# Half-size loads of the second half's token sums, and the final norm's weights in one VectorE operation, in a hybrid decoder layer

## The chip, the cores and the metric

The kernel runs on one core of a Trainium2 chip. The metric is the device time of one execution in microseconds (us). TensorE is called PE below, VectorE DVE (in the code `V`), ScalarE ACT (`A`), GpSimd POOL (`G`), and SyncE SP; SP issues nearly all DMA transfers. Each engine works through its own instructions in order, and semaphores tie the engines to each other.

## The reference

One decoder layer over 2048 tokens of 1024 features, all in float32. Its first part (a projection, gated linear attention on one group of heads, dilated sliding-window attention on the other, an output projection, residual) gives `h`. The change touches only what follows:

```python
nm = rmsnorm(h, mlp_norm_g[l])
a = jnp.square(jax.nn.relu(jnp.einsum('bsd,df->bsf', nm, w_ff1[l])))   # 1024 -> 4096
h = h + jnp.einsum('bsf,fd->bsd', a, w_ff2[l])                         # 4096 -> 1024
return rmsnorm(h, final_norm_g)       # x * rsqrt(mean(x^2) + 1e-6) * g
```

## The kernel before, in words

**Arithmetic.** Every float32 operand of a large matrix product is split in a high and a low part: `split` (L485 to L487) has ACT copy it to the high part (L486) and DVE subtract that from the original to get the low part (L487). `mm3` (L141 to L144) then adds three matmuls, high·high (L142), low·high (L143) and high·low (L144), each 128x128 by 128x512. The products are block products of Strassen's kind: sums and differences of blocks are formed first, so that a 2x2 block product takes seven multiplications in place of eight.

**MLP1** (L1280 to L1394). The 2048 tokens are worked in two halves. For each half there are 16 groups of 256 hidden features, and in each group seven products in the `order` 1, 2, 6, 5, 7, 3, 4; these 224 are the list `jobs1`. `prep1` forms and splits the weights of a job (tiles `w1raw`, `w1comb`), two jobs ahead. The other operand is one of seven token-sum blocks per half, which stay in SBUF as high and low tiles `hb` (`TF[j]`, each 128x2048) for all 16 groups of the half. A product is added up in a PSUM bank; `ps_a`, `ps_c`, `ps_d` and `ps_o` are the names of eight banks used in turn. When it is done, ACT copies the bank to SBUF (L1371, L1385) or DVE adds it to another (L1373, L1377, L1381), and ACT applies ReLU and square (L1362, L1363, L1386). `some_sums` adds the results for MLP2 on DVE (L1335) and SP stores these sums (L1337, L1368).

**The switch between the halves.** The `hb` tiles hold the seven blocks of one half only. Those of the second half were computed earlier and wait in DRAM (`hTD[1]`). During the last group of the first half (jobs from `first` = 7·15 = 105 on) block after block has been used for the last time, and its tiles are filled again: `reload` (L1246 to L1261) loads a whole block of 128x2048 (1 MB) into one of two `rb` buffers, and the generator that it returns splits the block in two halves of 1024 columns, each by `split`. `parts_at` says after which job each of the 14 half splits stands in the program. The loads of the first two blocks are issued at job `first` − 2, that of block n + 2 when both halves of block n have been split and so its buffer is free.

**MLP2** (L1432 to L1639). 26 products (`PRODUCTS`) of four steps each. Per step, `prep_a` loads and splits activation sums (`ra`, then `ca`; with a negative sign by L1458 and L1459), `prep_b` splits weight sums (`bs`, then `cb`), and `update_b` (L1490 to L1499) adds a freshly loaded weight block (`rb`) to `bs`, mostly on POOL (L1499). L1487 and L1497 load weights, L1446 activations. PE needs the split `ca` and `cb` of a step before its matmuls. `taken` (L1547 to L1561) adds a finished PSUM bank to the output tiles `sum` on DVE (L1556).

**The final norm** (`output`, L1510 to L1523) is called when an output row block of 128 tokens is complete, once for each of 16 row blocks, in four sets of four. A row block is two tiles of 128x512, `C[0]` and `C[1]`. ACT squares both with a running sum (L1515), POOL multiplies `C[0]` with the weights `g` (L1517), ACT makes the row factor `r` (L175, L176, L1518), DVE multiplies `C[1]` with `r` and `g` in one operation (L1520), ACT scales `C[0]` with `r` (L1521), and both tiles are stored (L1522, L1523). `last` is true for the last row block alone.

**Order of the work.** The program is written as above, and a scheduler of the tile framework puts each engine's instructions in their final order before the kernel runs. So an instruction added in one place can change the order of others on its engine; a wait follows from what an instruction reads and writes.

Of the kernel before, what the change touches and what calls it, by code (L numbers as in the profile page):

```python
# [13 lines left out]
AF = mybir.ActivationFunctionType  # L14
OP = mybir.AluOpType
# [101 lines left out]
def emit(tc, a, stop=99):  # L117
    nc = tc.nc
    V, A, G, T, SP = nc.vector, nc.scalar, nc.gpsimd, nc.tensor, nc.sync
# [6 lines left out]
    def ps(tag):  # L126
        return psum.tile([128, 512], F32, name="ps_" + tag, tag=tag, bufs=BANKS[tag])

    def slot(name, dt=F32, n=SLOT):

        return up.tile([128, SLOT], dt, name=name, tag="u", bufs=25)[:, :n]
# [34 lines left out]
    def stat(n=1):  # L166
        if stat_at[0] + n > 48:
            stat_at[0] = 0
        s = stats[:, stat_at[0]:stat_at[0] + n]
        stat_at[0] += n  # L170
        return s

    def rstd_of(ssq, width, n=1, bias=eps):
        r = stat(n)
        A.activation(r, ssq, AF.Ln, bias=bias, scale=1.0 / width)  # L175
        A.activation(r, r, AF.Exp, scale=-0.5)  # L176
        return r
# [46 lines left out]
    hTD = dram.tile([2, 7, 128, 4, 512], F32, name="hTD")  # L224
# [15 lines left out]
    CX, c11, c12, c21, c22, last = [t[:, GP * q:GP * q + GP] for t in acc for q in range(2)]  # L240
# [11 lines left out]
    order = (1, 2, 5, 6, 3, 4, 7)  # L252
# [4 lines left out]
    TF = {j: [slot(f"tb{j}", FR) for _ in range(2 if j < 7 else 1)] for j in order}  # L257
# [227 lines left out]
    def split(hi, lo, src):  # L485
        A.activation(hi, src, AF.Copy)  # L486
        V.tensor_tensor(lo, src, hi.bitcast(F32), op=OP.subtract)  # L487
# [109 lines left out]
    def reload(n):  # L597

        j, cs = order[n // 2], slice(1024 * (n % 2), 1024 * (n % 2) + 1024)
        t = (xp, bp)[n // 2 % 2][:, cs]  # L600
        SP.dma_start(t, nTD[j - 1].rearrange("p c s -> p (c s)")[:, cs])

        def rest():
            hi, lo = [v[:, cs] for v in TF[j]]
            tc.keep_in_program_order(A.activation(hi, t, AF.Copy))
            V.tensor_tensor(lo, t, hi.bitcast(F32), op=OP.subtract)
            if n + 4 < 14:
                back.append(reload(n + 4))

        return rest  # L610
# [121 lines left out]
    for at in range(7, len(jobs)):  # L732
        g = jobs[at][0]
# [419 lines left out]
    for pr in range(4):  # L1153
# [3 lines left out]
        for hh, br in seq:  # L1157
# [3 lines left out]
            first = len(units)  # L1161
# [62 lines left out]
    rb, TF, TB = [slot("rb")], {}, {}  # L1224
# [53 lines left out]
    order = (1, 2, 6, 5, 7, 3, 4)  # L1278
# [10 lines left out]
    def prep1(at):  # L1289

        if at >= len(jobs1):
            return
        g, j = jobs1[at]
        if not combs1:
            combs1.extend(view(c[:, 1024 * q:], (2, 4, 128)) for c in [slot("w1comb", FR) for _ in range(2)]
                          for q in range(2))
        r = raw1[g % 2]
        (a11, a12), (a21, a22) = [[r[:, 4 * k:4 * k + 4, n * 128:n * 128 + 128] for k in range(2)] for n in range(2)]
        c = combs1[at % 4]
        split(c[:, 0], c[:, 1], {1: a11, 2: a12, 6: a11, 5: a21, 7: a11, 3: a12, 4: a22}[j])  # L1300
        if j == 1:
            V.tensor_tensor(a21, a21, a22, op=OP.add)
            V.tensor_tensor(a11, a21, a11, op=OP.subtract)
        if j == 2:
            V.tensor_tensor(a12, a12, a11, op=OP.subtract)
        if j == 6:
            V.tensor_tensor(a11, a22, a11, op=OP.subtract)
        if j == 4:
            load_w1(g + 2)
# [80 lines left out]
    def some_sums(n=3):  # L1390

        for _ in range(n):
            while sums1 and next(sums1[0], 0) == 0:
                sums1.pop(0)  # L1394
# [5 lines left out]
    for at, t in enumerate(tiles):  # L1400
# [8 lines left out]
        p = [ps("a"), ps("a")]  # L1409
        parts_ = 2 if at < 2 else 1  # L1410
        for q in range(parts_):
            for n in range(2):
                cs = slice(n * 512, n * 512 + 512)
# [20 lines left out]
    raw_a, comb_a, raw_b, comb_b, state, fin = [], [], [], [], [], {}  # L1434
# [5 lines left out]
    def load_a(n):  # L1440

        if n < 2 * NPH:
            p, k = divmod(n, 2)
            if len(raw_a) < 2:
                raw_a.append(view(slot("ra"), (4, 512)))
            SP.dma_start(raw_a[n % 2], actD[AT[p], :, 4 * k:4 * k + 4].rearrange("p q h s -> p q (h s)"))  # L1446

    def prep_a(n):

        if n >= LAST:  # L1450
            return
        if len(comb_a) < 3:
            comb_a.append(view(slot("ca", FR), (2, 2, 512)))
        c, r = comb_a[n % 3], raw_a[n // 2 % 2][:, n % 2 * 2:n % 2 * 2 + 2]
        if PRODUCTS[n // 4][0] > 0:
            split(c[:, 0], c[:, 1], r)
        else:
            A.activation(c[:, 0], r, AF.Copy, scale=-1.0)  # L1458
            V.scalar_tensor_tensor(c[:, 1], r, -1.0, c[:, 0].bitcast(F32), op0=OP.mult, op1=OP.subtract)  # L1459
        if n % 2:  # L1460
            load_a(n // 2 + 2)
# [14 lines left out]
    def fetch_b(n):  # L1476

        if n >= LAST:
            return
        if not raw_b:  # L1480
            raw_b.extend(view(v[:, 1024 * e:], (2, 512)) for v in [slot("rb2") for _ in range(2)] for e in range(2))
        fetched[n] = []
        for op, k, m in PRODUCTS[n // 4][2]:
            if op != "=":
                v = raw_b[turns[0] % 4]
                turns[0] += 1
                SP.dma_start(v, w2_part(n, k, m))  # L1487
                fetched[n].append((op, v))

    def update_b(n, engines=(G, V)):  # L1490

        if n >= LAST:
            return
        v = state_of(n)
        for op, k, m in PRODUCTS[n // 4][2]:
            if op == "=":
                SP.dma_start(v, w2_part(n, k, m))  # L1497
        for e, (op, r) in enumerate(fetched.pop(n)):
            engines[e].tensor_tensor(v, v, r, op=OP.add if op == "+" else OP.subtract)  # L1499

    def prep_b(n):

        if n >= LAST:
            return
        if len(comb_b) < 3:
            comb_b.append(view(slot("cb", FR), (2, 2, 512)))
        v = comb_b[n % 3]
        split(v[:, 0], v[:, 1], state_of(n))

    def output(C, row, i, last=False):  # L1510

        scr = fin["scr"][:, 512 * (i % 2):512 * (i % 2) + 512]
        ss, part = stat(2), stat()
        for n in range(2):
            A.activation(scr, C[n], AF.Square, accum_out=ss[:, n:n + 1])  # L1515
            if n == 0:
                G.tensor_tensor(C[0], C[0], fin["g"][:, :512], op=OP.mult)  # L1517
                A.activation(part, ss[:, 0:1], AF.Copy, bias=EPS, scale=1.0 / D)  # L1518
        r = rstd_of(ss[:, 1:2], D, bias=part)
        V.scalar_tensor_tensor(C[1], C[1], r, fin["g"][:, 512:], op0=OP.mult, op1=OP.mult)  # L1520
        A.activation(C[0], C[0], AF.Copy, scale=r)  # L1521
        SP.dma_start(out2[row:row + 128, 512:], C[1])  # L1522
        (A if last else SP).dma_start(out2[row:row + 128, :512], C[0])  # L1523

# [58 lines left out]

    first, parts_at = 7 * (NP - 1), {}
    for n in range(14):
        parts_at.setdefault(first + 1 + n * 4 // 5, []).append(n // 2)
    halves, begun = {}, set()
    for at in range(7, len(jobs1)):
        if at == first - 2:
            halves.update({n: reload(order[n], 1) for n in range(2)})  # L1590
        prep1(at + 2)
        some_sums()
        product1(at)
        for n in parts_at.get(at, ()):
            next(halves[n])
            if n in begun and n + 2 < 7:
                halves[n + 2] = reload(order[n + 2], 1)
            begun.add(n)
        n = at + 6 - len(jobs1)
        if n == 0:  # L1600
            load_a(0)
        if 0 <= n < 4:
            fetch_b(n)
            update_b(n, (V, V))
        if n == 3:
            load_a(1)
        if n in (3, 5):
            prep_b(n // 2 - 1)
            prep_a(n // 2 - 1)
            fetch_b(n // 2 + 3)  # L1610
# [4 lines left out]
    for ph, (_, chained, _, _) in enumerate(PRODUCTS):  # L1615
# [3 lines left out]
        for k in range(4):  # L1619
            n = 4 * ph + k  # L1620
# [53 lines left out]
def build(nc, inputs, stop=99):  # L1674
    arrays, aps = {}, {}
    for name in _INS:
        arrays[name] = np.ascontiguousarray(inputs[name])
    arrays.update(_constants())
    for name, v in arrays.items():
        aps[name] = nc.dram_tensor(name, v.shape, mybir.dt.from_np(v.dtype), kind="ExternalInput").ap()  # L1680
    aps["out"] = nc.dram_tensor("out", (1, S, D), F32, kind="ExternalOutput").ap()
    with tile.TileContext(nc, schedule_with_timeline_sim=True) as tc:
        emit(tc, aps, stop)
    return arrays
# [10 lines left out]
```

## Time and profile before

| what | value |
|---|---|
| median of 3 runs | 2280.32 us (2277.76 to 2281.45) |
| the profiled execution | 2283.21 us |
| its span, first to last instruction | 2281.4 us |
| mean granted PE clock | 0.994 of full speed |
| DVE busy | 1630.4 us (71% of the span) |
| ACT busy | 1230.4 us (54%) |
| POOL busy | 544.3 us (24%) |
| L486, ACT, `hb` from `rb`, 14 splits | 1052 ns each (median) |
| L487, DVE, `hb` from `rb`, 14 splits | 1223 ns each (median) |
| L1521, ACT, 16 scalings | 711 ns each (median) |

A row of a timeline has the start in us, the duration in us, the engine, the line of the kernel, the operation, output and inputs, shapes and the count; a row with a count above 1 stands for neighbours taken together. In square brackets stands how long the engine was idle just before, and what ended it. Busy shares are averages over stages that have different limits, so what counts for the change are the rows at the places that it touches.

### The profile page before, as it was taken

The numbers are of one execution on the slowest core, as the hardware profiler recorded it, in microseconds if no ns is written. First come the engines' busy times: TensorE is split into PE (matmuls) and PEld (weight loads), VectorE is DVE, ScalarE is ACT, GpSimd is POOL, SyncE is SP. The second block draws the span as 40 slices with busy tenths as digits, with TensorE's granted clock in tenths as the row PEclk, the third lists the DMA queues.
The fourth block names the chain that finished last, engine by engine and source line by source line (L and its number), as shares of the span: only waits on it lengthen the run. The fifth ranks groups of instructions, "written<-read, shape, count | busy, mean of one in ns | idle before, by whom it ended". The sixth has DMA issues, their size and how long they took to land.

```text
span 2281.4 us, 35136 instructions
## 1 busy us (share of the span) xinstructions
PE 2249.2 (99%) x12508; PEld 1945.9 (85%) x12508; DVE 1630.4 (71%) x3065; ACT 1230.4 (54%) x2436; POOL 544.3 (24%) x482
## 2 busy tenths in 40 slices
PE   9999999999999999999999999999999999999998
PEld 8978998899999998888888887888888878888876
DVE  8788878766667676446777778777777577576778
ACT  6665436426877874234555556555555433333446
POOL 1210002024385672000000000000007562032465
PEclk9999999999999999999999999999999999999999
DMA  5458754776768864678544456555479988676775
GB/s 201 134 182 245 252 155 136 223 234 221 223 196 255 262 207 139 221 232 273 185 138 153 137 161 202 163 165 163 128 266 285 311 279 277 214 254 227 261 255 175
DMA packets 359920, 478.59 MB, mean 210 GB/s; under 512 B 19333, under 2 KB 268694, under 8 KB 347712
## 3 DMA queue, kind: packets, MB, share of 16 engines
q1 hardware_dynamic: 355246, 467.69, 63.6%
q0 software_dynamic: 4352, 8.39, 2.0%
q8 instruction: 98, 1.61, 0.3%
q14 instruction: 78, 0.64, 0.1%
q10 hardware_dynamic: 146, 0.27, 0.0%
HBM read 326.54 MB, written 154.44 MB: 211 GB/s over the span
## 4 chain that ended last, share of the span: by engine, by line
PE 84%; DMA 5%; POOL 3%; DVE 3%; issue 3%; ACT 2%; SPq 0%; POOLq 0%; ACTq 0%; DVEq 0%
PE ps_a L143 9%; PE ps_a L142 9%; PE ps_a L144 9%; PE ps_c L143 7%; PE ps_c L142 7%; PE ps_c L144 7%; PE ps_a L893 4%; PE ps_o L142 3%; PE ps_o L144 3%; PE ps_o L143 3%; PE ps_d L143 3%; PE ps_d L142 3%; PE ps_d L144 3%; PE ps_d L874 3%; PE ps_c L852 2%
## 5 line engine op out<-in xcount | busy, mean ns | idle before, releaser
L1499 POOL TENSOR_TENSOR bs<-bs,rb 128x1024 f32<-128x1024 f32 x72 | 217.7, 3031 | 1072.3 <-DMA actD<-ring 836.9
L486 ACT ACTIVATE cb<-bs 128x1024 fp32r<-128x1024 f32 x104 | 110.2, 1060 | 272.7 <-issue 116.2
L487 DVE TENSOR_TENSOR cb<-bs,cb 128x1024 fp32r<-128x1024 f32 x104 | 165.2, 1589 | 124.4 <-ACT cb L486 123.7
L487 DVE TENSOR_TENSOR w1comb<-w1raw,w1comb 128x512 fp32r<-128x512 f32 x224 | 153.8, 689 | 96.4 <-ACT w1comb L486 95.5
L486 ACT ACTIVATE w1comb<-w1raw 128x512 fp32r<-128x512 f32 x224 | 140.3, 628 | 81.6 <-PE ps_c L144 29.5
L865 ACT ACTIVATE pe<-pe,O 128x256 f32<-128x256 f32 (+1 forms) x384 | 156.5, 453 | 45.8 <-DVE O L864 42.3
L893 PE MATMUL ps_a<-v,pt 128*128 128x65 f32 x1200 | 178.5, 253 | 2.5 <-ACT pt L881 1.9
L893 PEld LDWEIGHTS ps_a<-v,pt 128*128 128x128 f32 x1200 | 175.4, 196 | 3.5 <-ACT pt L881 2.1
L874 PE MATMUL ps_d<-ident,pe 128*128 128x128 f32 x600 | 159.7, 279 | 0.0
L864 DVE CUSTOM_DVE_ANT_0 pe<-ps_c,nb 128x256 f32<-128x256 f32 (+1 forms) x384 | 126.3, 361 | 40.9 <-PE ps_d L874 18.3
L286 ACT ACTIVATE wcomb<-wraw 128x512 fp32r<-128x512 f32 (+2 forms) x119 | 90.0, 757 | 98.8 <-PE ps_a L143 34.5
L142 PE MATMUL ps_c<-hb,w1comb 128*128 128x512 f32 x336 | 131.0, 390 | 0.5 <-ACT xs L1371 0.5
L143 PE MATMUL ps_c<-hb,w1comb 128*128 128x512 f32 x336 | 130.9, 390 | 0.0
L144 PE MATMUL ps_c<-hb,w1comb 128*128 128x512 f32 x336 | 130.2, 390 | 0.0
L487 DVE TENSOR_TENSOR ca<-ra,ca 128x1024 fp32r<-128x1024 f32 x84 | 126.8, 1511 | 3.8 <-ACT ca L486 3.8
L142 PE MATMUL ps_c<-cb,ca 128*128 128x512 f32 x312 | 122.1, 391 | 0.0
L143 PE MATMUL ps_c<-cb,ca 128*128 128x512 f32 x312 | 122.0, 391 | 0.0
L144 PE MATMUL ps_c<-cb,ca 128*128 128x512 f32 x312 | 122.0, 391 | 0.0
L351 POOL TENSOR_TENSOR acc<-acc,misc 128x264 f32<-128x264 f32 (+1 forms) x32 | 38.7, 1221 | 313.1 <-DMA wraw<-w_in 200.3
L874 PEld LDWEIGHTS ps_d<-ident,pe 128*128 128x128 f32 x600 | 110.0, 187 | 0.1
L142 PE MATMUL ps_a<-wo,mT 128*128 128x512 f32 x256 | 101.4, 396 | 0.0
L1362 ACT ACTIVATE acc<-acc 128x512 f32<-128x512 f32 x96 | 60.7, 632 | 74.1 <-DVE acc L1381 44.0
(410 smaller groups left out, 7146.7 us busy)
## 6 DMA issues: line engine op xcount, KB each, us to landing
ra<-actD SPq DMA_DIRECT2D x52, 1024.0 KB, 7.3
actD<-ring SPq DMA_DIRECT2D x176, 256.0 KB, 2.5
rb<-w_ff SPq DMA_DIRECT2D x88, 512.0 KB, 6.1
bs<-w_ff SPq DMA_DIRECT2D x72, 512.0 KB, 6.1
w1raw<-w_ff SPq DMA_DIRECT2D x32, 1024.0 KB, 5.7
k<-kD SPq DMA_DIRECT2D x16, 1024.0 KB, 7.4
rb<-hTD SPq DMA_DIRECT2D x13, 1024.0 KB, 5.9
wraw<-w_in SPq DMA_DIRECT2D x48, 256.0 KB, 3.9
```

What stands on the lines that cost most here:

```text
L142: T.matmul(out, sh, mh, start=first, stop=False, **kw)
L143: T.matmul(out, sl, mh, start=False, stop=False, **kw)
L144: T.matmul(out, sh, ml, start=False, stop=last, **kw)
L286: A.activation(hi, src, AF.Copy, scale=sc)
L486: A.activation(hi, src, AF.Copy)
L487: V.tensor_tensor(lo, src, hi.bitcast(F32), op=OP.subtract)
L864: V.tensor_tensor_reduce(p, s, bias, scale=1.0, scalar=BIG, op0=OP.add, op1=OP.min, accum_out=nm)
L865: A.activation(p, p, AF.Exp, bias=nm, scale=-1.0)
L874: T.transpose(pb[:, i * 128:i * 128 + 128], src, ident)
L893: T.matmul(self.b.opsum[:, n % 4], self.pt[:, i * 128:i * 128 + 128], self.b.v[:, blk, cols], start=first, stop=last)
L1362: A.activation(v, v, AF.Relu)
L1499: engines[e].tensor_tensor(v, v, r, op=OP.add if op == "+" else OP.subtract)
```

## The change

Two things are changed.

First, the token sums of the second half are loaded in 14 pieces of 128x1024 (512 KB), two for each block, into the halves of the same two `rb` buffers. Four pieces are issued at job `first` − 3, and piece n + 4 when piece n has been split. The splits themselves, their order and the jobs after which they stand are the same.

Second, for all row blocks but the last, `C[0]` is no longer multiplied with `g` on POOL and scaled with `r` on ACT. One DVE operation multiplies it with both, as it is done for `C[1]`. That is 15 operations less on POOL, 15 less on ACT, and 15 more on DVE.

```diff
@@ output
             if n == 0:
-                G.tensor_tensor(C[0], C[0], fin["g"][:, :512], op=OP.mult)
+                if last:
+                    G.tensor_tensor(C[0], C[0], fin["g"][:, :512], op=OP.mult)
                 A.activation(part, ss[:, 0:1], AF.Copy, bias=EPS, scale=1.0 / D)
         r = rstd_of(ss[:, 1:2], D, bias=part)
         V.scalar_tensor_tensor(C[1], C[1], r, fin["g"][:, 512:], op0=OP.mult, op1=OP.mult)
-        A.activation(C[0], C[0], AF.Copy, scale=r)
+        if last:
+            A.activation(C[0], C[0], AF.Copy, scale=r)
+        else:
+            V.scalar_tensor_tensor(C[0], C[0], r, fin["g"][:, :512], op0=OP.mult, op1=OP.mult)
@@ the switch
     for n in range(14):
-        parts_at.setdefault(first + 1 + n * 4 // 5, []).append(n // 2)
-    halves, begun = {}, set()
+        parts_at.setdefault(first + 1 + n * 4 // 5, []).append(n)
+    piece = lambda n: rb[n // 2 % 2][:, 1024 * (n % 2):1024 * (n % 2) + 1024]
+
+    def load_piece(n):
+
+        if n < 14:
+            SP.dma_start(piece(n), hTD[1, order[n // 2] - 1][:, 2 * (n % 2):2 * (n % 2) + 2].rearrange("p c s -> p (c s)"))
+
     for at in range(7, len(jobs1)):
-        if at == first - 2:
-            halves.update({n: reload(order[n], 1) for n in range(2)})
+        if at == first - 3:
+            for n in range(4):
+                load_piece(n)
         prep1(at + 2)
         some_sums()
         product1(at)
         for n in parts_at.get(at, ()):
-            next(halves[n])
-            if n in begun and n + 2 < 7:
-                halves[n + 2] = reload(order[n + 2], 1)
-            begun.add(n)
+            cs = slice(1024 * (n % 2), 1024 * (n % 2) + 1024)
+            split(*[v[:, cs] for v in TF[order[n // 2]]], piece(n))
+            load_piece(n + 4)
```

In the program as the scheduler orders it, DVE's final-norm operations also stand elsewhere: before the change, three of the first set's four L1520 stand ahead of the splits of `cb` and `ca` for which PE waits after that set; with it, all eight multiplies of the set do.

## The prediction

> **What bounds the kernel now.** The page's busy shares come first, then what PE waited for over the whole run; the columns of the second view are total us, times, longest.
>
> ```profile
> PE 2249.2 (99%) x12508; PEld 1945.9 (85%) x12508; DVE 1630.4 (71%) x3065; ACT 1230.4 (54%) x2436; POOL 544.3 (24%) x482
> ...
> PE ps_a L143 <- DVE ca L487: 6.6, 4, 4.3
> ...
> PE ps_d L142 <- ACT xs L1371: 2.7, 1, 2.7
> PE ps_a L142 <- ACT xs L1371: 2.6, 1, 2.6
> ```
>
> PE is busy for 99% of the 2281.4 us span, and the change leaves its matmuls as they are (some change places). So a gain can come only from PE's holes. Three of these lines lie where the change works: two single waits for ACT's copy out of PSUM (L1371), and the waits for the split of `ca` on DVE (L487). The timeline of PE (start, duration, operation) shows their full price. The first two stand where MLP1's first half gives way to the second:
>
> ```profile
> 1370.35 0.39 PE L144 MATMUL ps_o<-hb,w1comb 128*128 128x512 f32 x1
> 1373.42 0.50 PE L142 MATMUL ps_d<-hb,w1comb 128*128 128x512 f32 x1 [2.68 <-ACT xs L1371]
> ...
> 1377.64 0.40 PE L144 MATMUL ps_d<-hb,w1comb 128*128 128x512 f32 x1
> ...
> 1393.99 0.39 PE L144 MATMUL ps_d<-hb,w1comb 128*128 128x512 f32 x1
> 1396.97 0.50 PE L142 MATMUL ps_a<-hb,w1comb 128*128 128x512 f32 x1 [2.59 <-ACT xs L1371]
> ...
> 1401.20 0.40 PE L144 MATMUL ps_a<-hb,w1comb 128*128 128x512 f32 x1
> ```
>
> The other two stand in MLP2, each shortly after a set of four final norms:
>
> ```profile
> 2175.76 0.39 PE L142 MATMUL ps_a<-cb,ca 128*128 128x512 f32 x1
> 2180.41 0.80 PE L143 MATMUL ps_a<-cb,ca 128*128 128x512 f32 x1 [4.26 <-DVE ca L487]
> ...
> 2186.39 0.39 PE L142 MATMUL ps_c<-cb,ca 128*128 128x512 f32 x1
> ...
> 2248.05 0.39 PE L144 MATMUL ps_c<-cb,ca 128*128 128x512 f32 x1
> 2248.27 0.39 PE L142 MATMUL ps_a<-cb,ca 128*128 128x512 f32 x1
> 2250.13 0.51 PE L143 MATMUL ps_a<-cb,ca 128*128 128x512 f32 x1 [1.47 <-DVE ca L487]
> ```
>
> A matmul normally starts 0.22 to 0.23 us after the one before (2248.05 to 2248.27). Gap 1 lasts 1373.42 − 1370.35 − 0.23 = 2.84 us, and the 11 starts after it take 4.22 us in place of 2.5: **4.56** in all. Gap 2: 2.75 idle, and 4.23 in place of 2.5: **4.48**. Gap 3: 4.42 idle, and the 14 starts from 2180.41 to 2186.39 take 5.98 in place of 3.18: **7.22**. Gap 4: **1.63**, at full pitch afterwards. An idle of 2.75 us or more is thus paid for once more at about half pitch, one of 1.63 is not. Together 17.9 us are to be had, 0.8% of the run.
>
> The Trainium skill, "TensorE: Matmul & The Clock Gate", section "HAM oscillation — how this bites in real kernels", puts the limit above which a pause slows the array at about 3.4 us. Gaps 1 and 2 (2.84 and 2.75 us idle) show the slow pitch below it, so the rows decide; by the page these two would hold 3.4 us less to win.
>
> **What ends gaps 1 and 2.** ACT, in order (a bracket is the idle time ahead of the row and what ended it):
>
> ```profile
> 1368.09 0.62 ACT L1362 ACTIVATE acc<-acc 128x512 f32<-128x512 f32 x1
> 1370.36 1.06 ACT L486 ACTIVATE hb<-rb 128x1024 fp32r<-128x1024 f32 x1 [1.66 <-DMA rb<-hTD]
> ...
> 1372.79 0.58 ACT L1371 ACTIVATE xs<-ps_d 128x512 f32<-128x512 f32 x1
> ...
> 1393.40 2.00 ACT L486 ACTIVATE hb<-rb 128x1024 fp32r<-128x1024 f32 x2 [2.86 <-DMA rb<-hTD]
> ```
>
> ACT stands at a split of token sums whose load has not landed, and the copy that frees PE's bank is queued behind it. The chain of waits has these two loads (start, time to landing), and DVE's timeline has the splits that free a buffer:
>
> ```profile
> 1364.73 5.27 DMA rb<-hTD
> ...
> 1386.75 6.62 DMA rb<-hTD
> ```
>
> ```profile
> 1362.35 2.35 DVE L487 TENSOR_TENSOR hb<-rb,hb 128x1024 fp32r<-128x1024 f32 x2
> ...
> 1367.77 1.22 DVE L487 TENSOR_TENSOR hb<-rb,hb 128x1024 fp32r<-128x1024 f32 x1
> ...
> 1383.77 1.22 DVE L487 TENSOR_TENSOR hb<-rb,hb 128x1024 fp32r<-128x1024 f32 x1
> ```
>
> **The change at the switch.** A piece is issued as soon as its own half is split: 1.1 us earlier than the whole block (1363.6, not 1364.73), and with 512 KB. No row has this 512 KB load. The nearest, from the page's DMA issues (KB each, median us to landing):
>
> ```profile
> hD<-mx SPq DMA_DIRECT2D x16, 512.0 KB, 3.0
> ...
> mx<-x SPq DMA_DIRECT2D x16, 512.0 KB, 6.3
> ...
> xp<-x SPq DMA_DIRECT2D x10, 512.0 KB, 4.2
> ```
>
> Bounds are 3.0 and 6.3; I take **4.2**, as it is also what the 5.27 of a whole block, less a part of its bytes, lies nearest to.
>
> The Trainium skill, "DMA: Bandwidth & Descriptors", section "Bandwidth", asks for transfers of 1 MiB or more, which speaks against halving them. The fit in its page "SBUF — State Buffer", section "The DMA setup-cost knee", gives 3.2 us for 512 KB as an estimate; with it the wait of 0.9 worked out below would vanish.
>
> Replayed with 4.2, in the order in which the built program has ACT (first half of the block waited for, L1362, second half, copy of ps_d): the halves land at 1363.6 + 4.2 = 1367.8 and 1364.7 + 4.2 = 1368.9, and ACT comes to them at 1368.1 and 1369.6 (1.0 and 0.5 us later by the pitches of L486 and L1362). The copy ends at about 1371.2 where PE would want it at 1370.6: **0.6** remains, at full pitch. New here: the first half of the next block now stands ahead of the copy of ps_o. Its piece follows the DVE row 1367.77, is issued at 1369.0 and lands at 1373.2; split and copy end at 1374.8. PE, 12 matmuls after 1371.2, asks at 1373.9: a new wait of **0.9**. At a landing of 3.0 it is none; at 6.3 it is 3.0, and with the slow pitch 4.7.
>
> For gap 2 the piece is issued when the DVE row 1383.77 ends, 1385.0, and lands at 1389.2, before ACT gets there (1393.40 − 2.86 = 1390.5). Then DVE is next:
>
> ```profile
> 1358.00:1378.00 20.00, 17.32 (x70) 13.86 (x69) 15.64 (x22) 13.15 (x20) 0.00 (x0) 0.91 0.53 171
> 1378.00:1402.00 24.00, 21.41 (x88) 17.19 (x87) 22.55 (x37) 17.62 (x27) 0.00 (x0) 0.93 0.70 227
> ```
>
> (Columns: length, busy us of PE, PEld, DVE, ACT, POOL, then the granted clock of PE: 0.91 and 0.93, the slow pitch again.) DVE has 15.64 + 22.55 = 38.2 us of work here, while PE needs 44 − 4.56 − 4.48 = 35.0. What is left over, 3.2 us, either becomes PE's wait or moves later; some of it are sums for MLP2 with no reader near. I put **1.9** (bounds 0 and 3.2). Sum at the switch: 9.04 − 0.6 − 0.9 − 1.9 = **5.6 saved** (bounds 9.0 at landing 3.0 with DVE's rest deferred; 0.5 at 6.3, where gap 1 keeps 2.4, ps_o costs 4.7 and 1.4 stays of gap 2).
>
> SP issues seven more loads; it has no work of its own to delay, but it is in order, and pieces stand behind MLP2's stores (L1337, L1368). The scheduler also changes places of some sums and splits at the passage to MLP2. Nothing is charged: PE runs there without a hole, and DVE has 13 us in 60 to spare.
>
> ```profile
> 1660.00:1720.00 60.00, 60.00 (x267) 49.71 (x266) 46.84 (x80) 33.48 (x49) 4.31 (x1) 1.00 0.85 288
> ```
>
> If that cover is gone, it costs what an order's shift is worth there, one split of 1.22 us or two.
>
> **The change in the final norm.** POOL, DVE and SP around gap 3:
>
> ```profile
> 2146.82 4.75 POOL L1499 TENSOR_TENSOR bs<-bs,rb 128x1024 f32<-128x1024 f32 x2 [6.49 <-DMA bs<-w_ff]
> ...
> 2165.27 7.91 POOL L1517 TENSOR_TENSOR sum<-sum,gf 128x512 f32<-128x512 f32 x4
> ```
>
> ```profile
> 2162.97 2.88 DVE L1520 SCALAR_TENSOR_TENSOR sum<-sum,stats,gf 128x512 f32<-128x512 f32 x1
> ...
> 2176.99 3.36 DVE L487 TENSOR_TENSOR ca<-ra,ca 128x1024 fp32r<-128x1024 f32 x1
> ```
>
> ```profile
> 2165.79 0.42 SPq L1497 DMA_DIRECT2D bs<-w_ff  x1
> ...
> 2168.23 0.42 SPq L1497 DMA_DIRECT2D bs<-w_ff  x1
> ```
>
> ```profile
> L1517 POOL TENSOR_TENSOR sum<-sum,gf x16: 1267/1739/2281, 2165.3 to 2274.2; 128x512 f32<-128x512 f32 x16
> ```
>
> ```profile
> L1520 DVE SCALAR_TENSOR_TENSOR sum<-sum,stats,gf x16: 739/1770/2895, 2163.0 to 2276.0; 128x512 f32<-128x512 f32 x16
> ```
>
> The DVE split takes 1.22 us alone and 3.36 beside POOL, and the norm's multiply 0.74 or 2.9; L1499 takes 2.4 (half of 4.75) or 3.3. The two engines exclude each other on these operations, so their lone durations add up. Out go four POOL multiplies ahead of `ca`, 4 × 1.27 = 5.1 us. In come five DVE multiplies ahead of it (the built order has all eight of the set before this `cb` and `ca`; before, three), 5 × 0.7 = 3.5. But POOL also comes sooner to its next two L1499, whose loads, issued at 2165.8 and 2168.2, land some 6 us later (6.49 idle for such a load above). From 2165.3, when POOL falls quiet: eight multiplies at 0.66 to 0.74 and four splits at 1.14 to 1.22 make 9.8, one of them already under way, and two L1499 make 4.8, together 14.6: `ca` ends at 2179.9, not 2180.35. I take **0.5 saved**. If only one L1499 gets in, 2.4 more; if POOL comes after the splits altogether, `ca` is ready at 2175.1, and the gap with its slow pitch is gone, 7.2 (upper bound); if a third gets in, 1.9 is lost (lower bound).
>
> Gap 4 is the same tie: DVE is without idle from 2231.45 on, six POOL multiplies (7.6) go and five DVE multiplies (3.5) come ahead of `ca`, which is late by 1.6. It closes: **1.6 saved** (bounds 0 and 1.75). ACT loses 15 scalings; off the path. In the tail three go from ACT and three multiplies come to DVE, behind the last PE result: 0, ± 0.6.
>
> **Sum:** 5.6 + 0.5 + 1.6 = 7.7. The profiled execution took 2283.21, so 2275.5; it lies 2.9 (0.13%) above the median 2280.32, from which the forecast is **2272.6**.
>
> **Rivals.** (a) Both of POOL's pair miss DVE's splits at gap 3: 6.7 more, 2265.9. For it: the splits would be through at 2175.1, so loads some 3 us later than I put them do it. Against: the landing above, and that DVE and POOL have met in nearly each of these rows. Chance 0.13. (b) Pieces take about 6, and the waits only move (0.5 + 0.5 + 1.6): 2277.7. For it: 512 KB rows of 6.1 to 6.3 exist, and four pieces may share the queues. 0.21, with the case that DVE's work takes back what the loads give. (c) Slower: loads at 8.5, the slowest whole block:
>
> ```profile
> DMA to landing us min/median/max: 4.9/5.9/8.5
> ```
>
> Then the half waited for lands at 1372.1, not 1370.0, and the last, with the shift of the first, at 1395, not 1393.4: +3.7 at the switch; with a third L1499 at gap 3 (+1.9) less 1.6, +4.0: 2284.3, and a third slow stretch at ps_o (1.7) 2286. It decides at 1370.0 − 1363.6 = 6.4 us of landing time. 0.09. The change does what it says in the built program; that is no rival.
>
> **How the numbers follow.** Forecast (2268 to 2276) 0.57, (a) 0.13, (b) 0.21, (c) 0.09. The range from 2265 to 2280.5 leaves out (c), a little of (b) and of (a). Measurement tells about 0.2%, 4.6 us, from no change: faster than 2275.8 has the forecast but a little, and (a): 0.70; same 0.22; slower 0.08.
>
> **What would show it.** In the changed profile: no wait of 2 us for L1371 and full pitch near 1371 and 1394; pieces landing in 3 to 5 us; a short wait at ps_o for ACT; `ca` after the first norm set still 3 to 4.5 us late with half pitch after it, and no wait at the second. Wrong would be: landings above 6, a wait for DVE's `w1comb` splits above 3 us, or gap 3 gone.

## The result, and the profile after

The changed kernel takes 2276.68 us (median of 17, 2273.26 to 2279.89), the kernel before, on the same chip, 2280.5 (2275.51 to 2283.78). The ratio is 0.9983 with a 95% interval of 0.9977 to 0.999: 3.8 us saved, between 2.3 and 5.2. The forecast was 2272.6, 7.7 saved, with a range of 2265 to 2280.5. The direction was right and the size half of what was forecast: 2276.68 lies in the stated range, but outside the 2268 to 2276 that the prediction gave its own forecast, and nearer to its rival (b), 2277.7. The first profiled execution took 2279.83 us with a span of 2278.1.

The page and PE's waits over the whole run of the changed kernel (total us, times, longest):

```profile
PE 2245.7 (99%) x12508; PEld 1941.4 (85%) x12508; DVE 1627.7 (71%) x3080; ACT 1221.2 (54%) x2421; POOL 520.0 (23%) x467
...
PE ps_a L143 <- DVE ca L487: 4.5, 3, 2.8
...
PE ps_d L143 <- DVE w1comb L487: 1.8, 2, 1.4
...
PE ps_d L142 <- ACT xs L1371: 1.0, 1, 1.0
```

The two long waits for L1371 are gone, one of 1.0 is left, and the wait for `ca` is smaller. But a wait for DVE's split of `w1comb` has come up, and most of its 1.8 us stands at MLP1's start, where no wait was forecast; 0.3 stand at gap 2. The timeline of PE at the four gaps:

```profile
1376.71 0.39 PE L144 MATMUL ps_o<-hb,w1comb 128*128 128x512 f32 x1
1378.07 0.50 PE L142 MATMUL ps_d<-hb,w1comb 128*128 128x512 f32 x1 [0.97 <-ACT xs L1371]
...
1380.70 0.39 PE L144 MATMUL ps_d<-hb,w1comb 128*128 128x512 f32 x1
1381.73 0.50 PE L142 MATMUL ps_o<-hb,w1comb 128*128 128x512 f32 x1 [0.65 <-ACT acc L1371]
...
1396.21 0.50 PE L143 MATMUL ps_d<-hb,w1comb 128*128 128x512 f32 x1 [0.32 <-DVE w1comb L487]
...
1399.72 0.50 PE L142 MATMUL ps_d<-hb,w1comb 128*128 128x512 f32 x1 [0.48 <-ACT acc L1371]
...
2177.58 0.39 PE L142 MATMUL ps_a<-cb,ca 128*128 128x512 f32 x1
2180.76 0.50 PE L143 MATMUL ps_a<-cb,ca 128*128 128x512 f32 x1 [2.79 <-DVE ca L487]
```

Gap 1 is 1.13 us (1378.07 − 1376.71 − 0.23) at full pitch, and the new wait at ps_o is there with 0.80 (0.6 and 0.9 were forecast). Gap 2 has shrunk to three holes of 0.5, 0.65 and 0.3, of which the first alone is a wait for DVE. Gap 3 is 2.95, followed by a slow stretch. Gap 4 is gone. DVE and POOL ahead of gap 3:

```profile
2170.75 0.74 DVE L1525 SCALAR_TENSOR_TENSOR sum<-sum,stats,gf 128x512 f32<-128x512 f32 x1
2171.41 2.90 DVE L1521 SCALAR_TENSOR_TENSOR sum<-sum,stats,gf 128x512 f32<-128x512 f32 x1
2174.23 2.88 DVE L1525 SCALAR_TENSOR_TENSOR sum<-sum,stats,gf 128x512 f32<-128x512 f32 x1
...
2179.49 1.21 DVE L487 TENSOR_TENSOR ca<-ra,ca 128x1024 fp32r<-128x1024 f32 x1
```

```profile
2171.31 2.45 POOL L1499 TENSOR_TENSOR bs<-bs,rb 128x1024 f32<-128x1024 f32 x1 [5.83 <-DMA bs<-w_ff]
2174.07 2.49 POOL L1499 TENSOR_TENSOR bs<-bs,rb 128x1024 f32<-128x1024 f32 x1 [0.31 <-DMA bs<-w_ff]
```

The two L1499 that were forecast to get in did: each stretched one multiply from 0.74 to 2.9 us, and `ca` ended at 2180.7.

To compare traces, what PE lost is added up below: what the distance between the starts of successive matmuls has over 0.227 us, summed over a stretch (a shorter distance does not count; the sums are good to 0.2 us). The stretches are counted from MLP1's first matmul: its first 60 us, the switch (270 to 345), the first norm set (1060 to 1125) and the second (from 1165 on). "Tail" is from the start of the last matmul to the end of the span. Three rows are executions of one program, the changed kernel: "pieces in pairs" turned out to be it (below).

| kernel | MLP1's start | switch | first set | second set | tail |
|---|---|---|---|---|---|
| before | 1.5 | 9.0 | 7.1 | 1.9 | 9.7 |
| before, again | 1.3 | 5.8 | 7.6 | 1.9 | 9.7 |
| pieces only | 2.6 | 4.2 | 5.6 | 1.3 | 9.2 |
| norm only | 1.5 | 5.0 | 4.3 | 0 | 8.3 |
| changed | 3.6 | 3.8 | 4.5 | 0 | 8.9 |
| changed, again | 3.5 | 4.2 | 5.5 | 0 | 8.9 |
| changed ("in pairs") | 3.1 | 4.1 | 0 | 0 | 8.3 |

### The profile page after: what moved, and what is told of

Read it like the earlier page. It is cut to its first block, busy times and chain, and to the rows that moved or that the text cites. A ratio compares the mean times of both kernels' runs of the same rounds, so it can differ in the third digit from the quotient of the medians.

```text
span 2278.1 us, 35114 instructions
## 1 busy us (share of the span) xinstructions
PE 2245.7 (99%) x12508; PEld 1941.4 (85%) x12508; DVE 1627.7 (71%) x3080; ACT 1221.2 (54%) x2421; POOL 520.0 (23%) x467
## 4 chain that ended last, share of the span: by engine, by line
PE 84%; issue 4%; DVE 4%; DMA 4%; POOL 3%; ACT 1%; SPq 0%; POOLq 0%; DVEq 0%; ACTq 0%
PE ps_a L143 9%; PE ps_a L144 9%; PE ps_a L142 9%; PE ps_c L142 7%; PE ps_c L143 7%; PE ps_c L144 7%; PE ps_a L893 4%; PE ps_o L144 3%; PE ps_o L142 3%; PE ps_o L143 3%; PE ps_d L143 3%; PE ps_d L142 3%; PE ps_d L144 3%; PE ps_d L874 3%; PE ps_c L852 2%
## 5 line engine op out<-in xcount | busy, mean ns | idle before, releaser
L1499 POOL TENSOR_TENSOR bs<-bs,rb 128x1024 f32<-128x1024 f32 x72 | 219.8, 3059 | 1080.8 <-DMA actD<-ring 833.4
L486 ACT ACTIVATE cb<-bs 128x1024 fp32r<-128x1024 f32 x104 | 110.3, 1060 | 286.7 <-issue 117.3
L487 DVE TENSOR_TENSOR cb<-bs,cb 128x1024 fp32r<-128x1024 f32 x104 | 158.9, 1528 | 127.8 <-ACT cb L486 127.4
```

## The experiments

The theory after the two first traces (A): the parts add up as the traces show them, 5 us won at the switch, 2.6 and 1.8 at the norm sets, 0.7 in the tail, and 2 lost at MLP1's start, where the early piece loads stand in the way of a weight load. It left a question: that makes 8 us, and 3.8 were measured. The changed trace also began MLP1 at 1076.1 us and not at 1071.8, with the same order of matmuls up to there; rival B took that for a part of the change.

**Pieces only.** The change to the loads alone, `output` as before.

> Only the loads in half pieces; the final norm as before the change. Theory A (the parts add up as the two traces show them: about 5 us won at the switch between MLP1's halves, 2 us lost at the start of MLP1, where the piece loads now stand just ahead of the second group's weight load): PE's waits at the switch together under 2.5 us without the slow pitch, a wait of about 1.4 us for DVE's w1comb split some 25 us after MLP1's start, gaps 3 and 4 as before; 3 us under the kernel before. Rival B (the 4.35 us by which the changed kernel is late before MLP1 belongs to the change, through where its loads stand): MLP1's start is again 4 us later than in the trace of before, and the time is that of before within 2 us. Rival C (the gain comes from the final norm alone): no gain, 0 plus or minus 1.

2277.11 us; ratio 0.999 (0.9981 to 0.9998), 2.3 us saved (0.5 to 4.3). The switch loses 4.2 and MLP1's start 2.6, as A has it, and MLP1 begins at 1072.8: B falls, the late start was of one execution. C does not fall. Its 0 ± 1 overlaps the interval, and in the traces the pieces win 2.4 at the switch (against 6.6, the mean of the first three traces with whole blocks) and lose 1.2 at MLP1's start (2.6 against a mean of 1.4). The norm sets, whose code is unchanged here, lost 5.6 and 1.3, less than in the trace of before, so the norm sets, too, differ between executions.

**Norm only.** The change to `output` alone.

> Only the final norm's multiply on DVE; the loads in whole blocks as before. Theory A: gaps 1 and 2 as before (2.8 us idle each, then the slow pitch), no 2 us at the start of MLP1, gap 3 about 3 us with a slow stretch, gap 4 gone, tail 0.7 shorter; 5 us under the kernel before (2.6 + 1.8 + 0.7). Rival B: MLP1 starts as in the trace of before within 1 us, since the loads are as before, and the time is 5 us lower. Rival C: 4 us lower, all of what was measured for the whole change.

2277.0 us; ratio 0.9984 (0.9974 to 0.9994), 3.6 saved (1.4 to 5.9), which leaves room for A's 5 and C's 4 alike. Gap 4 and part of gap 3 are gone, and the start of MLP1 loses nothing new. The surprise is the switch, whose code is that of the kernel before. PE's timeline:

```profile
1372.81 0.50 PE L142 MATMUL ps_d<-hb,w1comb 128*128 128x512 f32 x1 [2.25 <-ACT xs L1371]
1373.15 0.40 PE L143 MATMUL ps_d<-hb,w1comb 128*128 128x512 f32 x1
...
1394.46 0.50 PE L142 MATMUL ps_a<-hb,w1comb 128*128 128x512 f32 x1 [2.32 <-ACT xs L1371]
1394.80 0.39 PE L143 MATMUL ps_a<-hb,w1comb 128*128 128x512 f32 x1
```

The gaps are 2.40 and 2.47 (the brackets come out 0.15 lower), and the matmuls after them keep the full pitch: 5.0 us lost, not 9.0. So the first trace of before held more than each execution has.

**The kernel before, again.**

> The kernel before, profiled once more. Theory D (the measured gain is half of what the two traces show since the first trace of before caught gaps 1 and 2 with the slow pitch behind them, which the same code in the run of the norm alone did not have): PE loses 5 to 6 us at the switch, not 9, with idle times of 2.2 to 2.8 us in both gaps, and gap 3 stays as it was, 6 to 7 us. Rival (before always loses 9 us there, and the change loses as much elsewhere): again 9 us, slow pitch after both gaps.

```profile
1374.16 0.50 PE L142 MATMUL ps_d<-hb,w1comb 128*128 128x512 f32 x1 [2.28 <-ACT xs L1371]
...
1376.49 0.63 PE L144 MATMUL ps_d<-hb,w1comb 128*128 128x512 f32 x1
1376.91 0.63 PE L142 MATMUL ps_d<-hb,w1comb 128*128 128x512 f32 x1
...
1396.59 0.50 PE L142 MATMUL ps_a<-hb,w1comb 128*128 128x512 f32 x1 [1.48 <-ACT xs L1371]
```

5.8 us at the switch: gap 1 of 2.43 with the slow pitch (0.42 between 1376.49 and 1376.91), gap 2 of 1.64 without. An idle of 2.43 brought the slow pitch here and one of 2.47 did not in the run above. Theory D holds for the switch, though gap 2 is shorter than the 2.2 it named: at about 2.4 us the slow pitch came once and stayed away twice, and 3.45 of the 9.0 in the first trace were its price. The first norm set, though, lost 7.6 again.

**Loads late.** The changed kernel with its first four loads pinned in SP's order.

```diff
-                load_piece(n)
+                load_piece(n, tc.keep_in_program_order)
```

> The whole change, but the first four piece loads are pinned in SP's order behind what is traced ahead of them, so that they go out near the end of MLP1's first half and not at its start. Theory A: the wait for the w1comb split at the start of MLP1 falls from 1.4 to 0.3 us or less, the rest as in the changed kernel; 2 us under it, so 6 us under the kernel before. Rival (the second weight load is late for another reason): the wait stays above 1 us and the time is that of the changed kernel. A danger: block 0's pieces come too late for the switch; then a wait of over 1 us shows at the first split there.

2271.77 us; ratio 0.9962 (0.9948 to 0.9975), 8.7 under the kernel before and so more than A's 6, which lies at the edge of the interval. MLP1's start loses 1.3 and the wait for `w1comb` there is gone; the switch loses 3.8, so the loads do not come too late. Where the rest of the gain comes from the trace does not show: its execution took 2275.25, the longest of six, and lost 7.4 at the first norm set. Three timelines show why: SP and DVE of the kernel before, of the changed kernel, and of this one.

```profile
1080.94 0.32 SPq L1251 DMA_DIRECT2D rb<-hTD  x1
...
1087.01 0.32 SPq L1251 DMA_DIRECT2D rb<-hTD  x1
1087.61 0.38 SPq L1287 DMA_DIRECT2D w1raw<-w_ff  x1
...
1096.53 0.69 DVE L1302 TENSOR_TENSOR w1raw<-w1raw 128x512 f32<-128x512 f32 x1 [1.60 <-DMA w1raw<-w_ff]
```

```profile
1086.30 4.33 SPq L1596 DMA_DIRECT2D rb<-hTD  x3
...
1091.96 0.53 SPq L1596 DMA_DIRECT2D rb<-hTD  x1
1092.59 0.81 SPq L1287 DMA_DIRECT2D w1raw<-w_ff  x1
...
1102.31 0.69 DVE L1302 TENSOR_TENSOR w1raw<-w1raw 128x512 f32<-128x512 f32 x1 [3.67 <-DMA w1raw<-w_ff]
```

```profile
1088.19 0.39 SPq L1287 DMA_DIRECT2D w1raw<-w_ff  x1
...
1094.24 0.69 DVE L1302 TENSOR_TENSOR w1raw<-w1raw 128x512 f32<-128x512 f32 x1
```

The scheduler lifts the first loads of the second half's token sums to the first moment at which their buffer is free, 280 us ahead of their use. In the kernel before, one of two was out 6.7 us ahead of the second group's weight load; in the changed kernel all four pieces go out in the 6.3 us ahead of it, DVE has the weights 9.7 us after their issue and not 8.9, and DVE waits 3.67 for them. Without loads in the way DVE does not wait. The rival, another cause of the late weight load, falls.

**Norm after split.** The changed kernel; a norm multiply on DVE is queued behind the `cb` and `ca` splits traced ahead of it (four of the first set's multiplies, not eight, stand ahead of the split of gap 3).

```diff
+        with tc.issue_after(fin["a"].ins), tc.issue_after(fin["b"].ins):
+            V.scalar_tensor_tensor(C[1], C[1], r, fin["g"][:, 512:], op0=OP.mult, op1=OP.mult)
```

> The whole change, but each final-norm multiply on DVE is queued behind the cb and ca splits traced just ahead of it, so only four of the first set's eight multiplies stand ahead of the split that PE waits for. Theory A (gap 3 is DVE order: eight multiplies and POOL's two L1499 ahead of the split): ca ends at about 2175 or 2176 on the scale of the trace of before, gap 3 shrinks under 1.5 us without the slow pitch; 3 to 4.5 us under the changed kernel. Rival (gap 3 is set by POOL's L1499 or by a load and not by the order of the multiplies): gap 3 stays above 2.5 us and the time is that of the changed kernel.

2272.67 us; ratio 0.9972 (0.9961 to 0.9984): by the ratios 2.5 under the changed kernel, where A named 3 to 4.5, and the two intervals overlap. At the place of gap 3 PE now waits for nothing. But one step later it waits 0.26 for `ca`, and two steps later 2.40:

```profile
2178.59 0.50 PE L143 MATMUL ps_a<-cb,ca 128*128 128x512 f32 x1 [0.26 <-DVE ca L487]
2186.72 0.50 PE L143 MATMUL ps_a<-cb,ca 128*128 128x512 f32 x1 [2.40 <-DVE ca L487]
```

So the order of the multiplies has a part in gap 3, but it does not decide alone. With this order none of the four traces taken (this one and three below) has a wait at that place; with eight multiplies ahead, two of six have one (changed and norm only). And something else stands behind it. The ACT half of the `ca` that is late by 2.40 was ready at 2179.2, but DVE, busy without a pause, came to it at 2185.46, after three multiplies of 2.9 and a `cb` split of 3.41 beside POOL.

In the run with late loads it is POOL that waits. There DVE went through seven of its eight multiplies at 0.74 and the splits behind them at 1.22, until 2172.2. POOL's next L1499 began meanwhile and took 7.92 in place of 2.4. POOL, ACT and SP of that run:

```profile
2166.51 7.92 POOL L1499 TENSOR_TENSOR bs<-bs,rb 128x1024 f32<-128x1024 f32 x1 [6.34 <-DMA bs<-w_ff]
```

```profile
2181.81 1.06 ACT L486 ACTIVATE ca<-ra 128x1024 fp32r<-128x1024 f32 x1 [6.28 <-DMA ra<-actD]
```

```profile
2162.54 0.39 SPq L1497 DMA_DIRECT2D bs<-w_ff  x1
2174.46 0.39 SPq L1487 DMA_DIRECT2D rb<-w_ff  x1
2174.94 0.42 SPq L1446 DMA_DIRECT2D ra<-actD  x1
```

The buffer of the activation load (L1446) is free at 2172.2. SP issues it at 2174.94, because it stands in order behind a weight load (L1487) whose buffer POOL reads until 2174.43. It lands at 2181.8, DVE is idle for 5.02 ahead of the split, and PE waits 1.75 and 2.48, two steps after the place of gap 3.

**Update on DVE.** The changed kernel; POOL's weight sums beside the first set are formed on DVE.

```diff
-            update_b(n + 4)
+            update_b(n + 4, (V, V) if ph == 21 else (G, V))
```

> The whole change, and the weight sums that POOL forms beside the first norm set (L1499 in product 21) are formed on DVE. Theory A (gap 3 is DVE and POOL excluding each other on operations with two SBUF inputs): no DVE operation of the set takes over 1.3 us, although DVE has three more of 1.2 us; ca comes 2 to 3 us earlier, gap 3 falls under 1 us, 3 to 4 us under the changed kernel. Rival (DVE simply has too much to do there): the three more operations make ca later by up to 3.7 us, gap 3 above 4 us, slower than the changed kernel.

2274.41 us; ratio 0.997 (0.9958 to 0.9982). From 2157.8 to 2184 none of DVE's multiplies, splits and adds takes over 1.23 us:

```profile
2173.17 1.22 DVE L1499 TENSOR_TENSOR bs<-bs,rb 128x1024 f32<-128x1024 f32 x1
2174.30 0.75 DVE L1521 SCALAR_TENSOR_TENSOR sum<-sum,stats,gf 128x512 f32<-128x512 f32 x1
...
2178.09 1.22 DVE L487 TENSOR_TENSOR ca<-ra,ca 128x1024 fp32r<-128x1024 f32 x1
```

That is the mechanism of A: alone, 0.75 and 1.22; beside POOL, 2.9 and 3.4. PE does not wait for this `ca`. The set still loses 3.0 in two earlier places, since DVE's adds wait for their weights (5.78 us before the first) and hold up the splits of L1459 behind them; the rival's later `ca` at gap 3 did not come. By time the run does not stand apart from the changed kernel, whose interval overlaps.

**Late and split.** Both mends of the change together.

> Both mends of the change at once: the first piece loads pinned late, and the norm's multiplies queued behind the splits. Theory A: the two gains add up, 4.9 and 2.6 under the changed kernel: 7 us under it, 10 under the kernel before. Rival (both hide the same wait at gap 3, where a load of activations comes next): no faster than the better one of the two, 6 to 8 us under the kernel before.

2271.57 us; ratio 0.9965 (0.9953 to 0.9977): 8.0 under the kernel before (5.2 to 10.7) and no faster than loads late alone. The rival's 6 to 8 is the nearer, though A's 10 lies within the interval. 4.3 are still lost at the first set, but not for the load that the rival names: the ACT half of the late `ca` was ready at 2178.4, and DVE, without a pause, came to it at 2184.26, after three multiplies of 2.9 and a `cb` split of 3.42.

**Activation loads first.** As the last, and from product 21 on SP issues L1446 ahead of L1487.

```diff
+                prep_a(n + 2)
+                if n + 6 not in fetched:
+                    with tc.issue_after(fin["ra"].ins):
+                        fetch_b(n + 6)
```

> As the kernel with both mends, and from product 21 on SP issues the activation load (L1446) ahead of the weight loads (L1487) that wait for POOL. Theory A (after the mends, what is late at gap 3 is the activation load, stuck in SP's queue behind a weight load that waits for POOL): the wait for ca in the set's last step goes from 2.5 us to under 1 us; 1 to 3 us under the kernel with both mends. Rival (the load is not on the path, DVE's order is): no difference, or slower by 1 to 2 us, as the weight loads come later.

2268.5 us; ratio 0.995 (0.9938 to 0.9962), the fastest here, 11 us under the kernel before. SP, and the stretch around the first set (length, busy us of PE, PEld, DVE, ACT, POOL, granted clock); PE waits for nothing from 2140 to 2260:

```profile
2161.97 0.33 SPq L1446 DMA_DIRECT2D ra<-actD  x1
2162.35 0.43 SPq L1487 DMA_DIRECT2D rb<-w_ff  x1
```

```profile
2155.00:2182.00 27.00, 27.00 (x120) 22.34 (x119) 25.26 (x24) 14.75 (x25) 12.06 (x5) 1.00 0.81 283
```

The interval overlaps that of the kernel without it (from 0.9953 to 0.9962), but the wait of 2.4 that it aimed at is gone in its trace, and in that of the next run, which keeps this order. What took it away is not shown. The weight loads behind it go out later too, and only one of DVE's eight multiplies took 2.9 here, against four in the run before it: POOL met DVE less. No run moves the weight loads alone.

**Whole blocks in the fastest.** The last kernel with the loads as in the kernel before.

> The fastest version so far (norm multiplies behind the splits, activation loads ahead of weight loads on SP) with the loads of the token sums put back to whole blocks: what the half pieces are worth by themselves. Theory A: PE loses 5 to 6 us at the switch in place of 3.1, nothing more at the start of MLP1 than in the kernel before (1.5), and nothing at gaps 3 and 4: 2 to 3 us slower than the fastest version, some 9 under the kernel before. Rival (the slow pitch after gaps 1 and 2 comes in most runs): 5 us slower than the fastest version.

2269.7 us; ratio 0.9952 (0.994 to 0.9965). The switch loses 6.8 (gap 1 of 3.33 with the slow pitch, gap 2 of 1.76), 3.7 more than with pieces, but the times differ by 1.2 us and the intervals lie on each other. By the ratios the half pieces are worth 0.5 us, give or take 4; the runs do not tell it more closely.

**Changed, again, and pieces in pairs.** A second profile of the changed kernel; and the changed kernel with both pieces of a buffer issued after its second split in the text of the program:

```diff
-            load_piece(n + 4)
+            if n % 2:
+                load_piece(n + 3)
+                load_piece(n + 4)
```

> The changed kernel, profiled once more. Theory A: 3.4 to 4 us lost at the switch with no slow pitch, 2.5 to 3.5 us in MLP1's first 60 us, 4 to 5 us at gap 3, none at gap 4; MLP1 starts at 1071 to 1074 us, not at 1076. Rival B (the late start belongs to the change): it starts at 1076 again.

> The changed kernel with one difference in the loads: two pieces are issued together when both halves of the block before them in the buffer are split, as a whole block is in the kernel before; PE, ACT and DVE have the same order of instructions as in the changed kernel. Theory E (the gain at the switch comes from issuing the first half earlier, not from its size, since pieces take 5.2 us to land and whole blocks 5.4 to 5.9): PE loses at the switch as in the kernel before, 5 to 6 us, 1.5 to 2.5 us more than in the changed kernel. Rival (the smaller size brings it): PE loses 3.5 to 4 us there as in the changed kernel, since each piece lands sooner than a block.

The second is no experiment on the loads: a load waits only for the split of its own half, so the engines got the same order and the same waits, and SP still issued each piece as its half came free. It counts as a third trace of the changed kernel (2276.48 us; ratio 0.9977, 0.9968 to 0.9986). The repeat took 2276.16 and began MLP1 at 1072.7. The switch repeats (3.8, 4.2, 4.1), and so does MLP1's start (3.6, 3.5, 3.1). The first norm set does not: 4.5, 5.5 and 0. In the first, DVE meets POOL at the multiplies; in the second, the multiplies pass and the activation load is late; in the third, POOL's pair comes between the multiplies early enough, and nothing waits. POOL's pair starts when its weight loads land, and that was 1095.2, 1095.9 and 1091.4 us after MLP1's first matmul; DVE's own times differ as well.

**Pieces after both.** The changed kernel; the second half's piece is queued first on SP, so both wait for both splits.

```diff
+            if n % 2 and n + 4 < 14:
+                with tc.issue_after(load_piece(n + 4).ins):
+                    load_piece(n + 3)
```

> The changed kernel, but a buffer's two pieces are queued on SP so that the second half's piece goes first and the first half's right behind it, so neither goes out before both halves of the block before are split, as with a whole block. (The scheduler also moves some of ACT's and DVE's work at the switch, nearer to the order of the kernel before.) Theory E (the earlier issue brings the gain at the switch, for a piece takes nearly as long to land as a block): PE loses 5 to 7 us there, as in the kernel before, against 3.3 to 4.2 in the changed kernel. Rival (the smaller size brings it): 4 us or less.

2274.27 us; ratio 0.9983 (0.997 to 0.9995). The switch loses 4.8, between the two theories' numbers. Gap 1 is back at its full length, with the slow pitch:

```profile
1374.00 0.50 PE L142 MATMUL ps_d<-hb,w1comb 128*128 128x512 f32 x1 [2.90 <-ACT xs L1371]
```

Gap 2 stays away. So at gap 1 the earlier issue is what helps, as far as one trace shows it in which ACT's and DVE's orders also changed; at gap 2 it is not shown what does. The size alone brings little. Landing times at the switch (1340 to 1402 us), of the half pieces in the changed kernel and of the whole blocks in the kernel before, from four loads each:

```profile
DMA to landing us min/median/max: 5.0/6.0/6.6
```

```profile
DMA to landing us min/median/max: 4.9/5.9/6.6
```

## Why the prediction was right and wrong

**The number.** 2276.68 is nearest to rival (b), which had a chance of 0.21. Its condition held, and with it the prediction's own sign of being wrong, landings above 6: at the switch the pieces took 6.0 in the median and up to 6.6. Its account did not hold, for the switch still won 2.6 and not 0.5. That the range held is in part luck. By the traces the switch and MLP1's start brought 5.0 less than forecast and the norm sets and the tail 3.8 more, and these misses cancel in good part.

**Right: which holes PE has and what ends them.** All four were found and three moved as forecast. Gap 4 closed (1.6 forecast; 1.7 won as a mean over the second set's column). The remainders at gap 1 (0.6; 1.13, 0.82 and 1.28 in the three traces) and the new wait at ps_o (0.9; 0.80, 0.87 and 1.55) came, somewhat larger.

**Wrong, the main term: "Sum at the switch: 9.04 − … = 5.6 saved".** The 9.04 was one execution's price. 3.45 of it was the slow pitch after two gaps, which a second trace of the kernel before shows after one, and the same code in the norm-only run after none. Over three traces the switch cost 6.6 before and 4.0 after: 2.6. What was forecast to remain, 0.6 + 0.9 + 1.9 = 3.4, came near that 4.0; the price of before was too high. The Trainium skill, "TensorE: Matmul & The Clock Gate", section "What's actually happening", says that the activity window runs freely and does not start with the kernel; that fits a slow pitch after 2.43 us of idle and none after 2.47. The length of about 3.4 us that it gives for the window does not fit as a threshold, as the measurements lie below it.

**Wrong: the landing of a piece, "I take 4.2".** At the switch it was 6.0 in the median, against 5.9 for whole blocks: half the bytes saved nothing there. The piece that ended gap 1 in the first trace took 6.1 (issued at 1370.3; ACT's split of it started at 1376.47). The page of before also has weight loads of 512 KB on the same queue (`rb<-w_ff` and `bs<-w_ff`), and they take 6.1; the sum left them to rival (b). The 8.5 of rival (c) was likewise of another place, a load issued at 1027.8 us; the slowest whole block at the switch took 6.6. The gain at gap 1 came, as far as it is shown, from the other half of the argument, the earlier issue. The fit of the Trainium skill's page "SBUF — State Buffer", "The DMA setup-cost knee", from which 3.2 was estimated, is further off than the 4.2 taken from a row.

**Wrong: "SP issues seven more loads; it has no work of its own to delay".** The sum looked at the pieces' number and not at the place of the first four. They cost 2.0 at MLP1's start (1.4 before, 3.4 in the three traces of the changed kernel), shown by the run that moved them.

**Right in size, wrong in cause: DVE as the bound at gap 2, "I put 1.9".** The holes that stayed there add up to 1.4, 2.0 and 0.9 in the three traces of the changed kernel. But only 0.5, 1.1 and 0 of it was a wait for DVE's split of `w1comb`; for the rest PE waited for ACT.

**Half right: gap 3, "I take 0.5 saved".** That DVE and POOL exclude each other, and that the eight multiplies then delay `ca`, was so (2.9 for a multiply beside POOL in the changed trace, 0.74 alone). But the outcome is no number. It saved about 2.6, 1.6 and 7 in three executions. The wait at this place was gone in two of them, as rival (a) has it, but in one the activation load in SP's queue then cost as much two steps later. Neither that load nor a wait on POOL's side was in any step of the prediction.

**The tail** got shorter by 0.8, a little outside the 0 ± 0.6.

With the means of the traces the sum is −2.6 at the switch, +2.0 at MLP1's start, −3.4 and −1.7 at the norm sets, −0.8 in the tail: 6.5 saved (the switch of the norm-only run and the sets and tail of the pieces-only run counted with the kernel before). Measured were 3.8 (2.3 to 5.2) and, in ten more executions of the same program, 5.2 (3.2 to 7.3, from the ratio). Single executions of one program differ by 6 to 8 us, and two or three traces of each are a small sample of that. The trace that lost nothing at the first set is of the fastest of those ten executions (2270.34, median 2276.48), so to count it as one in three gives it too much weight. With the two other traces of the changed kernel alone the sum is 4.6 saved, an estimate from the table that lies in both intervals.

## What to carry to other kernels

A hole read in one trace is one draw: before it is entered as a term, ask which part of it hangs on a threshold (here the slow pitch after 2.2 to 2.6 us of idle) or on a race between two landings, and enter it as a range. When a load can be issued long before its use, look at where the scheduler really puts it and what it then stands in front of; pinning four loads later was worth 2 us in the traces, as much as most parts of the change. And behind a wait that is taken away, follow each queue one step further: in two traces the next thing late was an unrelated load, stuck on SP behind one that waited for POOL, and in two others DVE itself. And a row that shares only its bytes with a new load is a weak guide to its landing: rows of 512 KB lay anywhere from 3.0 to 6.3 us.

## What the runs showed of the hardware that was not expected

Halving a load from 1 MB to 512 KB took its median landing time only from between 5.4 and 5.9 us to between 4.7 and 5.6, over all runs; at the switch it was 5.9 before and 6.0 after. After an idle of PE of 2.2 to 2.6 us in MLP1 or MLP2 the slow pitch came or stayed away: it came after 2.16 (at MLP1's start in the run with the update on DVE), 2.43 and 2.58, and not after 2.40, 2.47 and 2.56. At 2.71 and above it came each time, and no idle of 1.9 or less brought it. DVE and POOL do not share time on operations with two SBUF inputs, one waits for the other's whole instruction: the multiply of 0.74 us took 2.9, POOL's L1499 of 2.4 took 7.92 while DVE went on, and with POOL's work moved away none of the set's operations was longer than alone.
